# Norm weights on the queries alone, roots as the sigmoids' scale, and one eviction per head, in a two-layer hybrid decoder trunk

## The chip, the cores and the metric

The kernel runs on one core of a Trainium2 chip. A core has several engines with a queue each, and each queue is worked off in order: TensorE (PE, matrix products; its weight loads are shown as PEld), VectorE (DVE), ScalarE (ACT), GpSimd (POOL) and SyncE (SP). An engine that waits for a semaphore holds up all that stands behind in its queue. Transfers run beside the engines on 16 DMA engines, fed by queues that belong to the engine that issues them. The metric is the device time of one execution in microseconds (us), smaller is better.

## The reference

Two layers, each `x + mix @ w_out`, with a residual stream of 512 tokens by 2048 channels in 32 bit. All three parts of a layer read one projection of the normalised input: a short convolution, stick-breaking attention, and gated linear attention (GLA). The change is in the attention, 8 heads of 128 channels, which is this:

```python
q = _rmsnorm(sb_q.reshape(b, s, SB_HEADS, SB_HD), sb_qn_g)   # mean of squares over 128, + EPS, times a weight
k = _rmsnorm(sb_k.reshape(b, s, SB_HEADS, SB_HD), sb_kn_g)
# per block of 128 queries, strictly causal:
z = (q * hd ** -0.5) @ k.T
log_keep = where(mask, log_sigmoid(-z), 0)
later = reverse_cumsum(log_keep) - log_keep
w = where(mask, exp(log_sigmoid(z) + later), 0)
y_sb = (w @ v) * silu(sb_g)
```

Since exp(log_sigmoid(z) + later) is a sigmoid times a product of sigmoids, the kernel computes sigmoid(z) and sigmoid(-z) and a running product of the latter. The weights of the two norms differ by channel (`sb_qn_g`, `sb_kn_g`), the inverse roots by token and head.

## The kernel before

All matrix products are carried by pairs of half-precision numbers, a high part and the rest, with three products for each (high by high, high by low, low by high). Every weight column block of 256 columns is loaded in 32 bit (`fetch`, L346 to L360, issued from GpSimd), squared and summed for a scale (`wmax`, L366 on ScalarE), and split into the two halves (L435 and L442, or L485 and L486 for the blocks that use a product scheme with seven smaller products, `project_quick`, L749). Those steps are given a high priority.

The attention is a loop over j = 0 to 3 (L1277), two heads a pass, in each layer. A pass projects the values, the gate, the queries and the keys for 256 columns. `project_gate` and the keys' projection use `project_quick`, whose parts leave PSUM in pieces (L778 to L792). For the queries and then the keys (L1298) the pass
- copies the projection to SBUF (`raw`; one buffer for the queries),
- sums the squares of each token and head on ScalarE (L1318, eight pairs of instructions),
- forms the inverse roots of eight columns on VectorE in `rsqrt_bits` (L208): the scaled sum (L211), a first guess by integer arithmetic (L213) and three Newton steps of three instructions (L216 to L218), and then a scaling by the projection's unit `u` (L1324),
- multiplies in place: the queries by their roots in one instruction (L1327), the keys by their roots and by the channels' weights `kg` in eight instructions, one for each token tile and head (L1332); `kg` holds both norms' weights, so the queries have none,
- splits the product into the two halves (`qp`, one buffer; L1336 on ScalarE, L1337 on VectorE) and transposes each by a DMA issued from SyncE (L1341).

`attend` (L1214) then appends four steps to a list: the scores of the two heads and their values. `go` (L1210) takes the next of them off the list at fixed places of the following pass (after its values, its gate, its queries and its keys), and after the last pass in the second half of the convolution (`conv_in` and `conv_out`, L1346). The scores of a head are in two PSUM chunks (`CHUNKS`, L40): the query tiles 3 and 2 with 512 and 384 columns, and the tiles 0 and 1 with 128 and 256. For each chunk there are the products (L1226), the mask on the diagonal blocks (L1230), sigmoid(-z) and sigmoid(z) over the whole chunk with a scale that is the same for all queries (`nzun`, `zun`; L1234, L1236), a running product for each tile (L1239), their product (L1241), the split (L1244, L1245) and the transposes (L1247). The values of a head accumulate in one PSUM bank (L1263), which is evicted in two halves, one for each chunk (L1270); there is one such bank. `mixsplit` (L866) splits the result and sends it to DRAM (L879), and `mixload` (L881, L887, on SyncE) brings it back, in six loads, when the last pass is over.

The order of the instructions on each engine isn't the order of the text. A planner runs the program on a clock of its own before it is built, and an engine takes the instruction that is ready on that clock, with the earlier in the text or the higher priority first. The first stage up to L655 alone is ordered by hand. On the chip that order is fixed: where a transfer takes longer than on the planner's clock, the engine waits.

Of the kernel before, what the change touches and what calls it, by code (L numbers as in the profile page):

```python
# [17 lines left out]
P = 128  # L18
# [18 lines left out]
TWICE = ("wm", "wgm", "wq", "ws", "wp", "vu", "bm", "bsmix", "gsmix", "lr", "xr0", "xrm", "xrt", "xtot", "xrstd", "xrs")  # L37


CHUNKS = ((((3, 0), (2, 512)), (3, 2)), (((0, 0), (1, 128)), (0, 1)))  # L40
# [3 lines left out]
def hybrid_trunk(ctx, tc, x, norm_g, w_in, conv_w, conv_b, sb_qn_g, sb_kn_g,  # L44
# [163 lines left out]
    def rsqrt_bits(dst, src, scale, n, tag):  # L208

        m = sm(n, tag + "rm")  # L210
        V.tensor_scalar(m, src, scale, EPS, ALU.mult, ALU.add)  # L211
        r = sm(n, tag + "r0")
        V.tensor_scalar(r.bitcast(I32), m.bitcast(I32), -0.5, float(0x5F375A86), ALU.mult, ALU.add)  # L213
        t = sm(n, tag + "rt")
        for i in range(3):
            V.tensor_tensor(t, r, r, ALU.mult)  # L216
            V.scalar_tensor_tensor(t, t, -0.5, m, ALU.mult, ALU.mult)
            V.scalar_tensor_tensor(dst if i == 2 else r, t, 1.5, r, ALU.add, ALU.mult)  # L218
# [68 lines left out]
    def layer_consts():  # L287
# [3 lines left out]
        for l in range(depth):  # L291
# [11 lines left out]
            V.tensor_scalar(gq[:, 0:1], gq[:, 0:1], gq[:, 1:2], 2.0 ** -10, ALU.mult, ALU.mult)  # L303
# [353 lines left out]
    for l in range(depth):  # L657
# [556 lines left out]
        def attend(j, qT, kT, vh, vl, vu, g, s_):  # L1214
# [3 lines left out]
            def scores(hh):  # L1218

                th[hh] = wk([P, 2, 10, P], "th", 2, F16)  # L1220
                for n, (qtiles, _) in enumerate(CHUNKS):
# [12 lines left out]
                    S.activation(a, z[:, :zw], AF.Sigmoid, scale=nzun[:, l:l + 1])  # L1234
                    w = wk([P, zw], "zw")
                    S.activation(w, z[:, :zw], AF.Sigmoid, scale=zun[:, l:l + 1])  # L1236
# [12 lines left out]
            def values(hh):  # L1249
# [17 lines left out]
                for n, (_, cols) in enumerate(CHUNKS):  # L1267
                    q0 = min(cols)
                    a = op[:, 2 * n:2 * n + 2, :]
                    V.scalar_tensor_tensor(y[:, q0:q0 + 2, :], a[:, ::-1, :] if cols[0] > cols[1] else a, vu[:, 1:2],  # L1270
                                           g[:, hh, q0 * P:(q0 + 2) * P].rearrange("p (t c) -> p t c", c=P),
                                           ALU.mult, ALU.mult)
# [4 lines left out]
        for j in range(4):  # L1277
# [20 lines left out]
            for gain in (None, kg[:, l, :]):  # L1298
                raw = []

                def dst():
                    raw.append(wk([P, NT, GW], *(("raw", 1) if gain is None else ("kT",))))
                    return raw[0]
# [6 lines left out]
                sq = sm(8, "qs")  # L1310
                for b in range(2):
# [4 lines left out]
                    for i in range(4):  # L1316
                        cs = slice(i * P, (i + 1) * P)
                        S.activation(e[:, cs], rb.rearrange("p a c -> p (a c)")[:, cs], AF.Square,  # L1318
                                     accum_out=sq[:, 4 * b + i:4 * b + i + 1])
# [4 lines left out]
                V.tensor_scalar(rs, rs, u, None, ALU.mult)  # L1324
                if gain is None:
                    r8 = raw.rearrange("p a (h c) -> p (a h) c", c=P)
                    V.tensor_tensor(r8, r8, rs.rearrange("p (a o) -> p a o", o=1).to_broadcast([P, 8, P]), ALU.mult)  # L1327
                else:
                    for t in range(NT):
                        for hh in range(2):  # L1330
                            rp = raw[:, t, hh * P:(hh + 1) * P]
                            V.scalar_tensor_tensor(rp, rp, rs[:, 2 * t + hh:2 * t + hh + 1], gain, ALU.mult, ALU.mult)  # L1332

                top = 2.0 ** 10 if gain is None else 1.0
# [4 lines left out]
                nT_ = wk([P, 2, NT, 2, P], "kT" if qkT else "qT", dt=F16)  # L1339
# [4 lines left out]
            attend(j, *qkT, vh, vl, vu, g, s_)  # L1344
# [86 lines left out]
```

## Time and profile before

| | us |
|---|---|
| median of 3 runs | 1716.04 (1715.94 to 1717.55) |
| the profiled execution | 1717.69 |
| its span, first to last instruction | 1715.9 |
| TensorE busy | 1669.9 |
| VectorE busy | 1331.3 |
| ScalarE busy | 1129.1 |
| GpSimd busy | 239.2 |

The span is one execution as the hardware profiler recorded it. A row of a view names the engine, the line of the kernel, the operation, what is written and read, and its shape; a wait is put down to what ended it. The granted clock is the share of its full clock that TensorE was given. Views used here: the page (busy shares), the list of waits, windows (busy time of each engine in a stretch), the order of time on one engine, and groups of instructions by line. A TensorE that is busy is not always at its peak: matmuls overlap, and their recorded durations do too.

### The profile page before, as it was taken

How to read it: one execution, taken by the hardware profiler on the slowest of the kernel's cores; microseconds unless marked ns; L12 is line 12 of the kernel's file. 1: busy time of each engine (PE TensorE's matmuls, PEld its weight loads, DVE VectorE, ACT ScalarE, POOL GpSimd, SP SyncE). 2: the span in 40 equal slices, each digit the busy share in tenths (PEclk: the TensorE clock that was granted, in tenths of full speed). 3: DMA queues.
4: the chain of work that ended last, by engine and by line, in shares of the span. 5: the costliest groups of instructions: out<-in, count | busy, mean ns of one | idle time of the engine just before them, and what ended most of it. 6: DMA issues, size and time to landing. Idle time of an engine off the chain costs nothing.

```text
span 1715.9 us, 36876 instructions
## 1 busy us (share of the span) xinstructions
PE 1669.9 (97%) x15642; PEld 1298.4 (76%) x15642; DVE 1331.3 (78%) x2327; ACT 1129.1 (66%) x1619; POOL 239.2 (14%) x286
## 2 busy tenths in 40 slices
PE   7999999999999989999989999999999999899999
PEld 5644548989898964799976455689898889548998
DVE  8975889877878767785688677997786888677883
ACT  7667677767666656666665676776765767565662
POOL 1211111111111111001122101121111111101110
PEclk9999999999999999999999999999999999999999
DMA  7233323566766686245543332446666667753441
GB/s 251 83 114 98 99 64 99 145 116 152 136 149 139 147 233 164 77 150 181 186 103 108 116 102 75 118 123 125 148 136 105 146 132 150 201 153 108 162 151 50
DMA packets 181478, 227.26 MB, mean 132 GB/s; under 512 B 94194, under 2 KB 141628, under 8 KB 180800
## 3 DMA queue, kind: packets, MB, share of 16 engines
q0 software_dynamic: 60352, 168.83, 34.4%
q1 hardware_dynamic: 111952, 46.61, 14.4%
q10 hardware_dynamic: 9008, 9.45, 1.7%
q8 instruction: 122, 2.00, 0.5%
q14 instruction: 44, 0.36, 0.1%
HBM read 179.65 MB, written 14.68 MB: 113 GB/s over the span
## 4 chain that ended last, share of the span: by engine, by line
PE 73%; DVE 12%; DMA 7%; ACT 4%; issue 3%; POOL 0%; DVEq 0%; ACTq 0%
PE psp L767 13%; PE psp L674 8%; PE psp L675 8%; PE psp L673 8%; PE psp L685 7%; PE psp L684 7%; PE psp L683 7%; PE psp L814 6%; PE psp L764 3%; DMA st<-in_w_in_dram 2%; DVE wl L486 2%; DMA th<-za 2%; DMA kT<-qp 2%; ACT junk L366 1%; DVE wl L442 1%
## 5 line engine op out<-in xcount | busy, mean ns | idle before, releaser
L366 ACT ACTIVATE junk<-st 128x2048 uint8<-128x2048 f32 x150 | 285.1, 1901 | 44.1 <-DMA st<-in_w_in_dram 42.8
L442 DVE SCALAR_TENSOR_TENSOR wl<-st,ws,wh 128x2048 f16<-128x2048 f32 x102 | 239.2, 2347 | 80.7 <-ACT wh L435 80.7
L435 ACT ACTIVATE wh<-st,ws 128x2048 f16<-128x2048 f32 x100 | 199.3, 1998 | 105.4 <-PE psp L674 47.1
L684 PE MATMUL psp<-wl,m 128*128 128x256 f16 x960 | 261.7, 273 | 0.0
L683 PE MATMUL psp<-wh,m 128*128 128x256 f16 x960 | 261.7, 273 | 0.0
L685 PE MATMUL psp<-wh,m 128*128 128x256 f16 x960 | 261.7, 273 | 0.0
L485 ACT ACTIVATE wh<-st,ws 128x1024 f16<-128x1024 f32 x150 | 167.6, 1143 | 120.5 <-DVE st L506 57.7
L486 DVE SCALAR_TENSOR_TENSOR wl<-st,ws,wh 128x1024 f16<-128x1024 f32 x150 | 189.6, 1279 | 27.4 <-ACT wh L485 27.3
L355 POOL DMA_DIRECT2D st<-in_w_in_dram x114 | 102.2, 900 | 436.0 <-DVE wl L442 319.4
L683 PE MATMUL psp<-wh,x 128*128 128x256 f16 x512 | 139.6, 273 | 0.0
L684 PE MATMUL psp<-wl,x 128*128 128x256 f16 x512 | 139.6, 273 | 0.0
L685 PE MATMUL psp<-wh,x 128*128 128x256 f16 x512 | 139.6, 273 | 0.0
L675 PE MATMUL psp<-x,wl 128*128 128x512 f16 x352 | 134.4, 382 | 2.2 <-DVE zun L186 2.2
L674 PE MATMUL psp<-x,wh 128*128 128x512 f16 x352 | 134.4, 382 | 0.0
L673 PE MATMUL psp<-x,wh 128*128 128x512 f16 x352 | 134.0, 381 | 0.0
L673 PE MATMUL psp<-m,wh 128*128 128x512 f16 x352 | 133.9, 380 | 0.0
L674 PE MATMUL psp<-m,wh 128*128 128x512 f16 x352 | 133.9, 380 | 0.0
L675 PE MATMUL psp<-m,wl 128*128 128x512 f16 x352 | 133.9, 380 | 0.0
L675 PEld LDWEIGHTS <-wl 128*128 128x128 f16 x704 | 69.2, 98 | 85.0 <-DVE wl L442 2.7
L673 PEld LDWEIGHTS <-wh 128*128 128x128 f16 x704 | 69.2, 98 | 81.5 <-issue 3.1
L380 POOL PARTITION_ALL_REDUCE wgm<-wm x75 | 40.0, 533 | 648.2 <-ACT junk L366 633.6
L674 PEld LDWEIGHTS <-wh 128*128 128x128 f16 x704 | 69.2, 98 | 80.8 <-issue 2.3
(427 smaller groups left out, 4042.2 us busy)
## 6 DMA issues: line engine op xcount, KB each, us to landing
st<-in_w_in_dram POOLq DMA_DIRECT2D x114, 1024.0 KB, 8.4
st<-in_w_out_dram POOLq DMA_DIRECT2D x32, 1024.0 KB, 7.4
st<-st POOLq DMA_DIRECT2D x18, 512.0 KB, 8.3
st<-in_w_in_dram SPq DMA_DIRECT2D x6, 1024.0 KB, 12.0
mixd<-g POOLq DMA_DIRECT2D x24, 256.0 KB, 7.7
x<-in_x_dram SPq DMA_DIRECT2D x4, 1024.0 KB, 4.9
qT<-in_x_dram ACTq DMA_DIRECT2D x8, 512.0 KB, 3.8
qT<-xs ACTq DMA_DIRECT2D x8, 512.0 KB, 3.9
```

What stands on the lines that cost most here:

```text
L366: sq = S.activation(junk(HK * GW).rearrange("p (k n) -> p k n", k=HK), staged[i][h], AF.Square, accum_out=peak[i][:, h:h + 1])
L435: hi = S.activation(wh[:, :, :GW], staged[i][h], AF.Copy, scale=scales[i])
L442: V.scalar_tensor_tensor(wl[:, :, :GW], staged[i][h], scales[i], wh[:, :, :GW], ALU.mult, ALU.subtract)
L485: hi = S.activation(h_, b, AF.Copy, scale=sc)
L486: V.scalar_tensor_tensor(l_, b, sc, h_, ALU.mult, ALU.subtract)
L673: T.matmul(o, wh[:, kk, cs], xh[:, :, k, :], start=st_, stop=False)
L674: T.matmul(o, wh[:, kk, cs], xl[:, :, k, :], start=False, stop=False)
L675: mm = T.matmul(o, wl[:, kk, cs], xh[:, :, k, :], start=False, stop=en)
L683: T.matmul(o, ah[:, t, k, :], wh[:, kk, :n], start=st_, stop=False, skip_group_check=True)
L684: T.matmul(o, ah[:, t, k, :], wl[:, kk, :n], start=False, stop=False, skip_group_check=True)
L685: return T.matmul(o, al[:, t, k, :], wh[:, kk, :n], start=False, stop=en, skip_group_check=True)
L767: mm = T.matmul(o[:, t * P:(t + 1) * P], a[p_][:, t, kk, :], w[q_][:, kk, :], start=st_, stop=en, skip_group_check=True)
```

## The change

It has four parts.

1. The norms' weights move from the keys to the queries. The queries are multiplied by `kg` alone, in one instruction for all heads and tiles (the same 128 columns repeated), and no longer by their roots. The keys are multiplied by their roots alone, also in one instruction.
2. The queries' inverse roots become the scale of the sigmoids, which is one number for each partition, and a partition of the scores is a query. Roots, unit and scale are put together in `qz`: eight columns for sigmoid(-z) and eight for sigmoid(z). The sigmoids are therefore taken tile by tile, four tiles a head, where they were taken by chunk. Constants of powers of two are shifted to keep the half-precision range (`2.0 ** -21`, `2.0 ** -14`, `2.0 ** 25`).
3. The scaled sums of queries and keys lie in one tile of 16 columns, and one Newton chain is run on it, when the keys' sums are there.
4. The second chunk of scores has its tiles in the order 1, 0, so that the four tiles of a head's values lie in the order 3, 2, 1, 0 in their bank, and one instruction evicts them.

```diff
-CHUNKS = ((((3, 0), (2, 512)), (3, 2)), (((0, 0), (1, 128)), (0, 1)))
+CHUNKS = ((((3, 0), (2, 512)), (3, 2)), (((1, 0), (0, 256)), (1, 0)))
...
-    def rsqrt_bits(dst, src, scale, n, tag):
-
-        m = sm(n, tag + "rm")
-        V.tensor_scalar(m, src, scale, EPS, ALU.mult, ALU.add)
+    def rsqrt_bits(m, tag):
+
+        n = m.shape[-1]
         r = sm(n, tag + "r0")
         V.tensor_scalar(r.bitcast(I32), m.bitcast(I32), -0.5, float(0x5F375A86), ALU.mult, ALU.add)
         t = sm(n, tag + "rt")
         for i in range(3):
             V.tensor_tensor(t, r, r, ALU.mult)
             V.scalar_tensor_tensor(t, t, -0.5, m, ALU.mult, ALU.mult)
-            V.scalar_tensor_tensor(dst if i == 2 else r, t, 1.5, r, ALU.add, ALU.mult)
+            V.scalar_tensor_tensor(r, t, 1.5, r, ALU.add, ALU.mult)
+        return r
...
-                    S.activation(a, z[:, :zw], AF.Sigmoid, scale=nzun[:, l:l + 1])
                     w = wk([P, zw], "zw")
-                    S.activation(w, z[:, :zw], AF.Sigmoid, scale=zun[:, l:l + 1])
+                    for m, dst in ((0, a), (8, w)):
+                        for t, o in qtiles:
+                            ts_ = slice(o, o + (t + 1) * P)
+                            S.activation(dst[:, ts_], z[:, ts_], AF.Sigmoid,
+                                         scale=qz[:, m + 2 * t + hh:m + 2 * t + hh + 1])
...
-                for n, (_, cols) in enumerate(CHUNKS):
-                    q0 = min(cols)
-                    a = op[:, 2 * n:2 * n + 2, :]
-                    V.scalar_tensor_tensor(y[:, q0:q0 + 2, :], a[:, ::-1, :] if cols[0] > cols[1] else a, vu[:, 1:2],
-                                           g[:, hh, q0 * P:(q0 + 2) * P].rearrange("p (t c) -> p t c", c=P),
-                                           ALU.mult, ALU.mult)
+                V.scalar_tensor_tensor(y, op[:, ::-1, :], vu[:, 1:2], g[:, hh, :].rearrange("p (t c) -> p t c", c=P),
+                                       ALU.mult, ALU.mult)
...
-            for gain in (None, kg[:, l, :]):
+            sq, rm = sm(16, "qs"), sm(16, "qrm")
+            for n in range(2):
...
                 V.tensor_scalar(u2, u, u, 1.0 / P, ALU.mult, ALU.mult)
-                rs = sm(8, "qr")
-                rsqrt_bits(rs, sq, u2, 8, "q")
-                V.tensor_scalar(rs, rs, u, None, ALU.mult)
-                if gain is None:
-                    r8 = raw.rearrange("p a (h c) -> p (a h) c", c=P)
-                    V.tensor_tensor(r8, r8, rs.rearrange("p (a o) -> p a o", o=1).to_broadcast([P, 8, P]), ALU.mult)
+                V.tensor_scalar(rm[:, 8 * n:8 * n + 8], sq[:, 8 * n:8 * n + 8], u2, EPS, ALU.mult, ALU.add)
+                r8 = raw.rearrange("p a (h c) -> p (a h) c", c=P)
+                if not n:
+                    qu = sm(1, "qu")
+                    V.tensor_scalar(qu, u, nzun[:, l:l + 1], 2.0 ** 25, ALU.mult, ALU.mult)
+                    by = kg[:, l, :].rearrange("p (o c) -> p o c", o=1)
                 else:
-                    for t in range(NT):
-                        for hh in range(2):
-                            rp = raw[:, t, hh * P:(hh + 1) * P]
-                            V.scalar_tensor_tensor(rp, rp, rs[:, 2 * t + hh:2 * t + hh + 1], gain, ALU.mult, ALU.mult)
+                    rs = rsqrt_bits(rm, "q")
+                    qz = sm(16, "qz")
+                    V.tensor_scalar(qz[:, :8], rs[:, :8], qu, None, ALU.mult)
+                    V.tensor_scalar(qz[:, 8:], qz[:, :8], -1.0, None, ALU.mult)
+                    V.tensor_scalar(rs[:, 8:], rs[:, 8:], u, None, ALU.mult)
+                    by = rs[:, 8:].rearrange("p (a o) -> p a o", o=1)
+                V.tensor_tensor(r8, r8, by.to_broadcast([P, 8, P]), ALU.mult)
+
+                top = 2.0 ** 10 if n else 2.0 ** -14
```

More of the change, by code (lines that the diff above doesn't have):

```diff
@@ L33 @@
 AHEAD = (8, 17, 21)
-TWICE = ("wm", "wgm", "wq", "ws", "wp", "vu", "bm", "bsmix", "gsmix", "lr", "xr0", "xrm", "xrt", "xtot", "xrstd", "xrs")
-CHUNKS = ((((3, 0), (2, 512)), (3, 2)), (((0, 0), (1, 128)), (0, 1)))
+TWICE = ("wm", "wgm", "wq", "ws", "wp", "vu", "bm", "bsmix", "gsmix", "lr", "xr0", "xrm", "xrt", "xtot", "xrstd", "xrs", "qz")
+CHUNKS = ((((3, 0), (2, 512)), (3, 2)), (((1, 0), (0, 256)), (1, 0)))
 @with_exitstack
@@ L1297, in hybrid_trunk @@
             qkT = []
-            for gain in (None, kg[:, l, :]):
+            sq, rm = sm(16, "qs"), sm(16, "qrm")
+            for n in range(2):
                 raw = []
                 def dst():
-                    raw.append(wk([P, NT, GW], *(("raw", 1) if gain is None else ("kT",))))
+                    raw.append(wk([P, NT, GW], *(("kT",) if n else ("raw", 1))))
                     return raw[0]
```

12 lines of the change are left out of this document (5 added, 7 removed).

## The prediction

> **What bounds the kernel now.** I read the page's busy shares first, then who TensorE waited for, then the windows around its two longest waits inside the attention, and last the queues that feed them (VectorE, ScalarE, SyncE) in order of time.
>
> ```profile
> span 1715.9 us, 36876 instructions
> ...
> PE 1669.9 (97%) x15642; PEld 1298.4 (76%) x15642; DVE 1331.3 (78%) x2327; ACT 1129.1 (66%) x1619; POOL 239.2 (14%) x286
> ```
>
> TensorE is busy for 97% of the span. What it loses is the difference, 46 us, and the change adds or removes no matmul. So the change is worth only what it does to TensorE's waits, of which these rows are the ones near it (total us, times, longest):
>
> ```profile
> PE psz L1226 <- DMA kT<-qp: 11.0, 2, 5.9
> PE psp L764 <- ACT g L785: 5.5, 6, 1.9
> ...
> PE psm L1263 <- DVE e L1270: 3.6, 1, 3.6
> ...
> PE psz L1226 <- ACT zw L1236: 1.4, 1, 1.4
> ```
>
> The first row is the scores' first matmul waiting for the transposed keys, once in each layer. The windows at these two places, two ordinary passes of the head loop, and the stretch before the first of the waits show what they cost (columns: length, busy time of each engine with counts, TensorE's granted clock, DMA share, GB/s):
>
> ```profile
> 594.40:624.00 29.60, 28.95 (x355) 25.96 (x353) 28.90 (x62) 22.02 (x38) 6.01 (x8) 1.00 0.75 181
> 1265.00:1350.00 85.00, 82.95 (x910) 75.09 (x908) 64.81 (x116) 52.65 (x81) 14.04 (x15) 1.00 0.79 147
> 634.28:640.15 5.87, 0.00 (x1) 0.00 (x1) 0.35 (x1) 0.00 (x0) 0.00 (x0) 0.86 1.23 159
> 640.15:645.35 5.20, 5.20 (x14) 1.85 (x14) 0.00 (x0) 1.06 (x1) 0.00 (x0) 0.50 0.93 317
> 1487.06:1492.22 5.16, 0.00 (x1) 0.00 (x0) 1.50 (x1) 0.00 (x0) 0.00 (x0) 0.96 1.21 193
> 1492.22:1495.30 3.08, 3.08 (x9) 1.17 (x9) 0.00 (x0) 0.00 (x0) 0.00 (x0) 0.51 1.03 291
> 420.00:505.00 85.00, 84.73 (x937) 76.92 (x935) 68.46 (x120) 58.66 (x89) 14.21 (x16) 1.00 0.68 147
> ```
>
> An ordinary pass has little to give: TensorE is busy 84.73 or 82.95 of 85.00 us, at a clock of 1.00. At the last pass (j = 3) of each layer TensorE stands still for 5.87 and 5.16 us, and then runs at half clock for 5.20 and 3.08 us, which loses another 5.20 x 0.50 + 3.08 x 0.49 = 4.1 us. Together 15.1 us: that is the prize. The Trainium skill, "TensorE: Matmul & The Clock Gate" (section "Why this matters for your kernels"), asks for no idle gap over about 3 us, since a longer one brings the half clock. The trace agrees here: both gaps are longer and both have it. By that rule a gap cut to under 3 us would save its clock part whole. The rows say so without it: the pass from 1265 loses 2.05 us in short waits and keeps its clock of 1.00.
>
> **Why the keys are late.** VectorE in the last pass of layer 0: the queries' product (L1327), the keys' Newton chain from its start (L211) to its end (L1324), a weight split (L442) that got in ahead, and the keys' eight products (L1332); under it the keys' products of layer 1.
>
> ```profile
> 597.01 0.17 DVE L218 SCALAR_TENSOR_TENSOR qr<-qrt,qr 128x8 f32<-128x8 f32 x1
> 597.21 0.17 DVE L216 TENSOR_TENSOR qrt<-qr 128x8 f32<-128x8 f32 x1
> ...
> 598.68 1.23 DVE L1327 TENSOR_TENSOR raw<-raw,qr 128x1024 f32<-128x1024 f32 x1
> ...
> 612.48 0.22 DVE L211 TENSOR_SCALAR qrm<-qs,qu 128x8 f32<-128x8 f32 x1
> ...
> 616.63 0.23 DVE L1324 TENSOR_SCALAR qr<-qr,wu 128x8 f32<-128x8 f32 x1
> 616.77 2.35 DVE L442 SCALAR_TENSOR_TENSOR wl<-st,ws,wh 128x2048 f16<-128x2048 f32 x1
> 619.03 2.19 DVE L1332 SCALAR_TENSOR_TENSOR kT<-kT,qr,kg 128x128 f32<-128x128 f32 x8
> ...
> 1471.80 2.18 DVE L1332 SCALAR_TENSOR_TENSOR kT<-kT,qr,kg 128x128 f32<-128x128 f32 x8
> ```
>
> ScalarE at that time: the last square of the keys, two weight splits with a copy between, the squares of the next weights, which wait 2.87 us for their DMA, and behind them the keys' half-precision copy (L1336).
>
> ```profile
> 610.51 0.29 ACT L1318 ACTIVATE e<-kT 128x128 f32<-128x128 f32 x1
> ...
> 612.96 1.14 ACT L485 ACTIVATE w7h<-st,ws 128x1024 f16<-128x1024 f32 x1
> ...
> 614.61 1.99 ACT L435 ACTIVATE wh<-st,ws 128x2048 f16<-128x2048 f32 x1
> 616.50 0.36 ACT L782 ACTIVATE qT<-psp 128x256 f32<-128x256 f32 x1
> 617.17 2.00 ACT L435 ACTIVATE wh<-st,ws 128x2048 f16<-128x2048 f32 x1 [0.31 <-PE psp L764]
> 622.05 1.91 ACT L366 ACTIVATE junk<-st 128x2048 uint8<-128x2048 f32 x1 [2.87 <-DMA st<-in_w_in_dram]
> ...
> 623.96 1.04 ACT L1336 ACTIVATE qp<-kT 128x1024 f16<-128x1024 f32 x1
> ```
>
> And SyncE, which issues the transposes: the queries' pair, four loads of the mix (two at 617.17, two at 622.41), the keys' two transposes; the last row is, over all of L1341's transposes, the time from issue to landing.
>
> ```profile
> 601.02 6.51 SPq L1341 DMA_TRANSPOSE qT<-qp  x2
> ...
> 617.17 0.94 SPq L887 DMA_DIRECT2D m<-mixd  x2
> ...
> 622.41 1.85 SPq L887 DMA_DIRECT2D m<-mixd  x2
> ...
> 625.02 8.40 SPq L1341 DMA_TRANSPOSE kT<-qp  x1
> ...
> 633.52 4.84 SPq L1341 DMA_TRANSPOSE kT<-qp  x1
> ...
> DMA to landing us min/median/max: 3.3/8.3/15.0
> ```
>
> The reader is to see a queue of three: the products end at 621.22, the copy at 625.00, and the two issues take 8.40 and 4.84 us, because the big mix loads have just gone into the same queue. The keys are there at 640.15; TensorE's order has the scores at 634.28. That place is the planner's estimate: it lies 13.06 us behind the products' end (634.28 - 621.22), and in layer 1 13.08 us (1487.06 - 1473.98).
>
> **The change, part by part.**
>
> *Queries' chain dropped, one chain of 16.* In each of the 8 passes VectorE loses ten small steps at a pitch of 0.20 us (597.01 to 597.21), 2.0 us, and one scaling by u, 0.23. The squared unscale and the scaled sums stay, one instruction each for queries and keys. Added are the queries' u (one column) and two rows of qz: at the 0.23 of L1324 at most 0.7. The queries' product still waits for its squares, because it writes over what they read; only the chain between is gone. So the queries go to SyncE about 2 us earlier, at some 599 instead of 601.02, and the copy of the keys, which needs their single buffer back, is released 2 us earlier. ScalarE's wait for that buffer (18.6 us in all) shrinks, beside TensorE's work:
>
> ```profile
> L1336 ACT ACTIVATE qp<-kT 128x1024 f16<-128x1024 f32 x8 | 8.4, 1053 | 21.8 <-DMA qT<-qp 18.6 <-DVE kT L1332 3.2
> ```
>
> *Keys' eight products become one.* 2.19 becomes the 1.23 of L1327 (same shape): 0.96 less. VectorE in all: 2.0 + 0.23 + 0.96 - 0.7 = 2.5 us a pass, 20 us of 1331. By itself this is hidden behind TensorE, worth nothing in passes 0 to 2.
>
> *What it does in pass 3.* VectorE is busy 28.90 of the 29.60 us before 624, so 2 us taken out at 597 come out of the backlog in front of 612.48. The squares end at 610.9 (610.51 + 0.29 and the read of the sum); the chain starts there, 1.6 us earlier, needs 2.0 us, the three small scalings 0.7, and I allow 0.4 for another step slipped in: about 614.0. The next weight split is ready at 612.96 + 1.14 = 614.10, so the keys' product runs just before or just after it: 614.0 + 1.23 = 615.2, or with a split of 1024 columns ahead of it (half of L442's 2.35 and a little, 1.3) 616.6. It ends between 615.2 and 616.6 instead of 621.22, in front of L442 either way. The copy then fits on ScalarE behind L782 (616.86) or behind the second L435 (619.17), and ends at 618 to 620.3, ahead of the squares that wait for a DMA. SyncE has issued the first two mix loads by 618.11 and its third is not ready before 622.41, so the planner should put the keys' transposes between them. Then they meet an emptier queue, as the queries did: second issue 1.6 us behind the first (6.51 us for both is the upper bound), 8.3 us to land, hence 628 to 630. The scores stand 13.06 us behind the product, at 628.3 to 629.7. A wait of 0 to 1.7 us is left; I take 1.5 a layer. Bounds from both sides: none left, and with the longest landing (15.0) 7 us, which is the present wait and more. The two mix loads that are now passed start up to 6.5 us later. Their first reader comes 60 us on, which covers that:
>
> ```profile
> L1150 ACT ACTIVATE m<-m,ratio x14: 706/1133/1148, 685.7 to 1543.4; 128x1024 f16<-128x1024 f16 x12, 128x512 f16<-128x512 f16 x2
> ```
>
> *Sigmoids.* Two chunks of 896 and 384 columns become four tiles of 512, 384, 256 and 128, twice each:
>
> ```profile
> L1236 ACT ACTIVATE zw<-psz,zun 128x896 f32<-128x896 f32 x16 | 16.0, 999 | 0.0
> ...
> L1236 ACT ACTIVATE zw<-psz,zun 128x384 f32<-128x384 f32 x16 | 9.4, 586 | 0.0
> ```
>
> 999 - 586 = 413 ns over 512 columns is 0.81 ns a column, and 0.28 us are fixed; four more instructions a head cost 1.1 us, or 0.7 where they overlap by 0.10 (614.61 + 1.99 against 616.50). Over 16 heads that is 11 to 18 us of ScalarE, which has 58.66 of 85 us filled. On TensorE's path it matters where a copy or a bank waits behind sigmoids: the seven waits of L785 and L1236 above. Each longer by 0.7 is 4.9 us, none longer is 0. The rows don't tell how many of L785's hang on sigmoids; with ScalarE two thirds full I take the lower third, 1.5. The rule that speaks against the change is in the Trainium skill, "ScalarE: Activation LUTs" (section "What ACT_TABLE_LOAD costs"): about 186 ns fixed, 93 more for a pointer operand. The trace agrees (0.28 with one). By the page's figure the four cost 4 x 0.28 x 16 = 17.9 us, which is the upper end above.
>
> *Values evicted at once.*
>
> ```profile
> L1270 DVE SCALAR_TENSOR_TENSOR e<-psm,vu,g 128x256 f32<-128x256 f32 x32 | 13.9, 477 | 10.2 <-ACT e L1318 8.4 <-PE psm L1263 1.8
> ...
> L877 DVE SCALAR_TENSOR_TENSOR g<-e,bsmix,g 128x512 f16<-128x512 f32 x12 | 8.9, 744 | 0.0
> ```
>
> 13.9 / 16 = 0.87 us a head become about the 0.74 of a 512-wide step. The bank is free when the last half is read, in both versions; the first half could start earlier before, but only the end counts. Between -3.6 (TensorE's wait for it gone) and +0.5 (the 477 ns of the half that can no longer run early), I take 0. The turned order of the last two tiles moves no work.
>
> **Sum.** Waits -11.0 + 3.0; clock -4.1; sigmoids +1.5; the rest 0: -10.6 us. The profiled execution took 1717.69 (span 1715.9 and 1.8 around it) and lies 1.65 above the median of 1716.04; taken off the median, **1705.5 us**.
>
> **Rivals.**
>
> *The wait stays.* The copy still ends up behind the squares, or the planner keeps all four mix loads first. SyncE is then free at 622.41 + 1.85 = 624.26, 0.76 us earlier than 625.02. For it: L366 is high in the planner's order and blocks ScalarE in both layers. Against it: the product comes over 4 us earlier. 1716 - 1.5 + 1.5 = 1716 us.
>
> *Slower: the scores move up, the transposes don't.* TensorE's order follows the planner's clock, not the chip's. If it moves the scores up with the product (to about 629) while on the chip the keys land at 640.15 - 0.76 = 639.4, the wait is about 10 us instead of 5.87, and 9.5 instead of 5.16: +8.7, and up to 3 more at half clock. It decides against the change as soon as the scores move up by more than 0.76 us without the transposes passing the mix loads. For it: the planner's 13.06 us were 5.87 too short already. With the sigmoids 1716 + 8.7 + 3 + 1.5 = 1729 us; half of that move gives 1722.
>
> *ScalarE eats the gain.* All of the 0.7 to 1.1 us a head reaches TensorE: 11 to 18 instead of 1.5, so 1715 to 1722 us. For it: ScalarE runs in order, with TensorE's copies behind the sigmoids. Against it: an ordinary pass leaves it 26 us idle.
>
> **Chances.** Forecast 0.50 (its own range 1698 to 1711: from all 15.1 and part of the L1270 wait gone, to half the waits left); wait stays 0.22; scores move up 0.16; ScalarE 0.12. A difference of 0.2%, 3.4 us, is about what a measurement of this kernel can tell from none. Faster: 0.50 and 0.05 of the two rivals near 1716, whose other waits shift with a new order: 0.55. Same 0.18, slower 0.16 and 0.11 of those two: 0.27. Leaving out no more than 2 in 10, the range runs from 1697 to 1724.
>
> **What would show it.** Right: the wait of L1226 for the transposed keys goes from 11.0 to under 4 us, the clock stays at 1.00 in the last passes, SyncE's keys stand between the second and the third mix load, L1336 for keys waits less than 18.6 us for the queries' transposes, VectorE is some 20 us less busy and ScalarE 11 to 18 more. Wrong: that wait unchanged or longer, or new waits of TensorE on sigmoids.

## The result, and the profile after

The changed kernel took 1739.28 us (median of 4 runs, 1737.37 to 1747.79), the kernel before beside it 1715.99 (4 runs, 1714.73 to 1717.55): ratio 1.0145, 95% interval 1.011 to 1.018. It is 23 us slower; 11 us faster was forecast. A later series gave 1743.30 and 1.0147 [1.0123, 1.0172].

The page of the changed kernel's profiled execution (1737.37 us), span and busy shares:

```profile
span 1735.6 us, 36801 instructions
...
PE 1672.7 (96%) x15642; PEld 1298.0 (75%) x15642; DVE 1311.7 (76%) x2191; ACT 1140.0 (66%) x1683; POOL 239.8 (14%) x286
```

VectorE has 19.6 us less to do and ScalarE 10.9 more, as forecast (20; 11 to 18). TensorE does the same work in 2.8 us more, and idles 62.9 us of the span instead of 46.0. So the loss lies in its waits. The view of waits, TensorE's rows of the attention (total us, times, longest):

```profile
PE psz L1226 <- DMA kT<-qp: 29.2, 4, 12.6
...
PE psp L764 <- ACT g L785: 3.7, 4, 1.5
...
PE psz L1226 <- ACT zw L1238: 2.3, 1, 2.3
...
PE psm L1266 <- DVE e L1270: 0.6, 1, 0.6
```

The wait that was to fall from 11.0 to 3.0 us rose to 29.2; of the others shown, the score banks' (1.4 before) rose by 0.9 us and two fell. In a second profile of the same kernel (e17 below) two of them are larger: 7.4 us for the score banks and 5.1 for the eviction. Windows around its three long pieces and behind two of them (columns as in the prediction: length, busy times, granted clock, DMA share, GB/s):

```profile
631.31:641.86 10.55, 0.00 (x1) 0.00 (x0) 1.27 (x1) 0.00 (x0) 0.00 (x0) 0.70 1.04 179
641.86:647.86 6.00, 5.99 (x20) 2.41 (x20) 0.00 (x0) 0.00 (x0) 0.00 (x0) 0.68 1.47 184
1391.25:1396.85 5.60, 0.00 (x1) 0.00 (x0) 0.00 (x0) 0.00 (x0) 0.00 (x0) 0.98 1.40 79
1494.19:1506.77 12.58, 0.01 (x1) 0.01 (x1) 2.35 (x1) 0.58 (x1) 0.00 (x0) 0.69 1.14 178
1506.77:1512.77 6.00, 6.00 (x15) 2.23 (x15) 0.00 (x0) 0.00 (x0) 0.00 (x0) 0.51 0.95 200
```

The two old gaps, 5.87 and 5.16 us, are 10.55 and 12.58, and layer 1's third pass has a new one of 5.60. In layer 0 the scores stand at 631.31, 2.97 us earlier than before, and the keys come at 641.86, 1.71 later. SyncE in that pass, in order of time:

```profile
597.01 9.93 SPq L1343 DMA_TRANSPOSE qT<-qp  x2
617.87 0.99 SPq L887 DMA_DIRECT2D m<-mixd  x2
621.45 3.16 SPq L1343 DMA_TRANSPOSE kT<-qp  x1
624.71 6.79 SPq L887 DMA_DIRECT2D m<-mixd  x2
631.59 12.95 SPq L1343 DMA_TRANSPOSE kT<-qp  x1
```

The planner put one of the keys' transposes between the second and the third mix load, as the prediction had it, and the other behind the fourth. Neither met an emptier queue: the second took 12.95 us to issue, and the first, which TensorE's wait was for, landed only 20.38 us after its issue. The chain in order of time (start, us):

```profile
621.45 20.38 DMA kT<-qp
```

The queries' pair now goes out 4.0 us earlier (597.01 against 601.02) and takes 9.93 us instead of 6.51. VectorE between the keys' squares and their product:

```profile
612.16 0.27 DVE L1321 TENSOR_SCALAR qrm<-qs,qu 128x8 f32<-128x8 f32 x1 [0.88 <-ACT e L1317]
...
613.59 1.28 DVE L486 SCALAR_TENSOR_TENSOR w7l<-st,ws,w7h 128x1024 f16<-128x1024 f32 x1
...
614.87 0.74 DVE L877 SCALAR_TENSOR_TENSOR g<-e,bsmix,g 128x512 f16<-128x512 f32 x1
...
616.03 2.35 DVE L442 SCALAR_TENSOR_TENSOR wl<-st,ws,wh 128x2048 f16<-128x2048 f32 x1
...
619.11 1.22 DVE L1334 TENSOR_TENSOR kT<-kT,qr 128x1024 f32<-128x1024 f32 x1
620.25 2.34 DVE L442 SCALAR_TENSOR_TENSOR wl<-st,ws,wh 128x2048 f16<-128x2048 f32 x1
```

And ScalarE, with the squares of the next weights ahead of the keys' last square:

```profile
609.85 1.90 ACT L366 ACTIVATE junk<-st 128x2048 uint8<-128x2048 f32 x1
...
611.74 0.29 ACT L1317 ACTIVATE e<-kT 128x128 f32<-128x128 f32 x1
```

The chain begins late, because it waits for that square, and three larger steps slip into it. The product ends at 620.33, 0.9 us earlier than before and not 4.6 to 6. Two more rows bear on the rest. The first, of VectorE's waits, is 0.3 us in the kernel before. The second is ScalarE's copy of the keys in layer 1's third pass, waiting for the queries' late transposes to give their buffer back, from which the new gap of 5.60 us follows:

```profile
DVE st L506 <- DMA st<-st: 9.2, 4, 5.9
```

```profile
1386.40 1.06 ACT L1338 ACTIVATE qp<-kT 128x1024 f16<-128x1024 f32 x1 [12.10 <-DMA qT<-qp]
```

The st wait is for L503, which adds one quarter of a weight block to another by a transfer in GpSimd's queue, behind the weight loads. It now lands late: at most 22.0 us after its issue, against 14.7 before.

### The profile page after: what moved, and what is told of

Same layout as the page of the kernel before. It is cut to its first block, busy times and chain, and to the rows that moved or that the text cites. A ratio compares the mean times of both kernels' runs of the same rounds, so it can differ in the third digit from the quotient of the medians.

```text
span 1735.6 us, 36801 instructions
## 1 busy us (share of the span) xinstructions
PE 1672.7 (96%) x15642; PEld 1298.0 (75%) x15642; DVE 1311.7 (76%) x2191; ACT 1140.0 (66%) x1683; POOL 239.8 (14%) x286
## 4 chain that ended last, share of the span: by engine, by line
PE 78%; DVE 8%; DMA 7%; ACT 4%; issue 2%; POOL 0%; ACTq 0%; DVEq 0%; POOLq 0%
PE psp L767 15%; PE psp L684 8%; PE psp L685 8%; PE psp L683 8%; PE psp L675 8%; PE psp L674 8%; PE psp L673 8%; PE psp L814 6%; PE psp L764 4%; DMA kT<-qp 2%; DMA st<-in_w_in_dram 2%; ACT junk L366 2%; PE psm L1266 1%; DVE wl L486 1%; PE psz L1014 1%
## 5 line engine op out<-in xcount | busy, mean ns | idle before, releaser
L366 ACT ACTIVATE junk<-st 128x2048 uint8<-128x2048 f32 x150 | 285.1, 1901 | 33.7 <-DMA st<-in_w_in_dram 32.5
```

Source lines behind the costliest of these rows:

```text
L366: sq = S.activation(junk(HK * GW).rearrange("p (k n) -> p k n", k=HK), staged[i][h], AF.Square, accum_out=peak[i][:, h:h + 1])
```

## The experiments

In each, the edit is against the kernel named. Ratios are against the kernel before, run beside it on the same chip; 0.001 is 1.7 us. "kT" is TensorE's wait for the transposed keys, "st" VectorE's wait for L503, both in the profiled run. The series ran on different chips, so between them only ratios are compared. One profile is one execution, and not always near the median: e10's (1699.62 us) is its fastest run, e13's (1726.89) close to its slowest. Line numbers shift by a few with the edits.

| run | kernel | median us | ratio, 95% interval | kT us | st us |
|---|---|---|---|---|---|
| | before | 1715.99 | 1 | 11.0 | 0.3 |
| | changed | 1739.28 | 1.0145 [1.011, 1.018] | 29.2 | 9.2 |
| e17 | changed, again | 1743.30 | 1.0147 [1.0123, 1.0172] | 27.4 | 13.8 |
| e1 | before + tiled sigmoids | 1727.35 | 1.0054 [1.0032, 1.0076] | 14.0 | 0.3 |
| e2 | before + single eviction | 1719.15 | 1.0009 [0.9987, 1.0031] | 12.9 | 0.6 |
| e3 | changed, queries' own chain | 1741.16 | 1.0138 [1.0104, 1.0172] | 28.2 | 0.5 |
| e4 | changed, keys' pair before 3rd mix load | 1748.63 | 1.0177 [1.0144, 1.0209] | 34.1 | 11.5 |
| e5 | changed, keys' pair before all mix loads | 1726.41 | 1.0052 [1.0027, 1.0077] | 5.8 | 9.2 |
| e6 | e5, weight load behind the pair | 1720.72 | 1.0014 [0.9993, 1.0035] | 5.2 | 10.5 |
| e13 | changed, keys' pair behind 4 mix loads | 1719.57 | 1.0015 [0.999, 1.0039] | 10.4 | 8.1 |
| e11 | e6 + queries' own chain | 1709.84 | 0.9968 [0.9942, 0.9993] | none | none |
| e16 | e13 + queries' own chain | 1712.76 | 0.9969 [0.9951, 0.9987] | 2.6 | none |
| e9 | before, keys' pair before all mix loads | 1712.64 | 0.9969 [0.9944, 0.9994] | 6.8 | 0.3 |
| e7 | e9, weight load behind the pair | 1704.74 | 0.9916 [0.989, 0.9941] | none | none |
| e14 | e7, again | 1699.90 | 0.9901 [0.9876, 0.9926] | none | none |
| e10 | e7 + tiled sigmoids | 1708.18 | 0.995 [0.9921, 0.9979] | none | none |
| e15 | e7, queries sent early | 1720.29 | 1.0024 [0.9997, 1.0051] | 7.1 | 16.4 |

### Parts of the change alone

e1: in the kernel before, each sigmoid cut into tiles, with the common scale kept:

```diff
-S.activation(a, z[:, :zw], AF.Sigmoid, scale=nzun[:, l:l + 1])
+for t, o in qtiles:                       # and the same for w with zun
+    ts_ = slice(o, o + (t + 1) * P)
+    S.activation(a[:, ts_], z[:, ts_], AF.Sigmoid, scale=nzun[:, l:l + 1])
```

> The kernel before with one part of the change alone: sigmoids tile by tile (eight a head), with the old scale. Theory order (the loss of 23 us comes from TensorE's scores moving up while the keys' transposes land later, at the last pass of each layer): within 4 us of before, 1712 to 1720, the wait for transposed keys stays at about 11 us in 2 waits. Theory sigmoids (the extra ScalarE time reaches TensorE): 1727 to 1734, with new waits of TensorE on L785 or on the score banks.

1.0054: the sigmoids alone cost some 9 us. The median lies at the lower edge of the second theory's range, but not by the waits that it named. TensorE's:

```profile
PE psz L1226 <- DMA kT<-qp: 14.0, 2, 8.4
PE psm L1265 <- DVE e L1272: 6.7, 3, 2.8
PE psp L764 <- ACT g L785: 5.4, 6, 1.6
```

The waits on L785 (5.5 before) and on the score banks (1.4 before, none here) did not grow; those for the values' eviction (3.6 before) and for the keys did.

e2: the kernel before with the values' tiles in the new order, evicted by one instruction for both halves (`V.scalar_tensor_tensor(y, op[:, ::-1, :], ...)` instead of the loop over CHUNKS):

> The kernel before with the turned tile order and the single eviction alone. Theories order and collision: 1712 to 1720, the wait for the eviction (3.6 us before) 0 to 4 us. Theory eviction (a later release of the bank holds up the values): over 1722, with waits of TensorE on L1270 above 6 us.

1.0009: nothing that could be measured, as forecast.

### The keys' transposes and the mix loads

e4, in the changed kernel (`order(a, b)` puts a behind b on the same engine; `turned` holds the last pass's two transposes):

```diff
 for i in range(2):
-    nc.sync.dma_start(mix[i][:, :, ks, :], mixd[l][...])
+    back_ = nc.sync.dma_start(mix[i][:, :, ks, :], mixd[l][...])
+    if i or ks.start == 4:
+        for a in turned:
+            order(back_, a)
```

> The changed kernel with both transposes of the last pass's keys held together in SyncE's queue ahead of the third mix load. Theory order (the second transpose is late because two mix loads stand before it): it is issued at about 624 instead of 631.6 of layer 0, the two last-pass waits fall from 10.6 and 12.6 to under 6 each, 1720 to 1728. Theory collision (a transpose that is in flight with weight loads crawls, wherever it stands): its issue or landing still takes over 10 us and the waits stay above 8 each, 1733 to 1742.

1.0177: exactly the place that the prediction gave the pair, unsplit, and the slowest of all, above both ranges. The waits are those of theory collision (15.5 and 18.1 us at the two last passes). Its SyncE, and its wait:

```profile
625.17 0.99 SPq L888 DMA_DIRECT2D m<-mixd  x2
628.75 16.13 SPq L1348 DMA_TRANSPOSE kT<-qp  x2
644.98 9.27 SPq L888 DMA_DIRECT2D m<-mixd  x4
```

```profile
PE psz L1230 <- DMA kT<-qp: 34.1, 3, 18.1
```

The third to sixth mix loads had not been issued, and still the pair took 16.13 us to issue. So these loads are not what holds it there, and the splitting of the pair is not needed for the loss.

e5 is e4 without its `if`: all six mix loads behind the pair. e6 adds to e5 that the one weight load that would run beside the pair waits for it, since two of its elements are first written from the transposed keys:

```diff
 whole[i] = stage.tile([P, KT, GW], F32, tag="st", name=nm("st"))
+if i in (29, 67):
+    G.tensor_copy(whole[i][0:1, HK - 1:HK + 1, 0], held[-1][0:1, 1, 0, 0, 0:2])
```

> The changed kernel with the last pass's two keys' transposes held ahead of all six mix loads of the layer in SyncE's order, nothing else. Theory 1 (collision: transposes in flight together with the 2 MB weight load of GpSimd's queue make both crawl): they are issued by about 622 and 624, the weight load of 622.9 is in flight with them, both take 15 us or more, the waits for kT at the two last passes stay between 25 and 36 us together, time 1736 to 1750. Theory 2 (it is the mix loads in the same queue that hold the transposes, as the prediction had it): with nothing ahead of them they land by 630 to 632, the two waits fall below 8 us together, time 1712 to 1722.

> The same with one more edit: the weight load that would be in flight with the last pass's keys' transposes (both halves of it, one load a layer) first has two of its elements written by GpSimd from the transposed keys, so it can only be issued once they have landed. Theory 1: the transposes, alone, take about 4 us each as in the passes without a collision and land at 628 to 632; the waits for kT at the two last passes fall from about 30 to under 10 us together, the weight load takes 6 to 11 us instead of 21 and is in no later than 644, time 1715 to 1726. Theory 2: the same waits as without the edit, and the weights later on top, time no lower than the kernel without it. A third case: the transposes land early, and TensorE then waits for the later weights (L442 or L435 as the releaser) for as long as it gained.

e5, 1.0052: theory 2's waits (5.8 us), and a time between the two theories'. With nothing before them the two issues take 3.55 us together instead of 16.13, and the first transpose is there when TensorE comes for it, in layer 0. The second is not through before the weights flow: it lands 11.61 us after its issue. SyncE, and the chain in order of time:

```profile
639.13 3.55 SPq L1347 DMA_TRANSPOSE kT<-qp  x2
...
641.44 11.61 DMA kT<-qp
```

e6, 1.0014: holding the weight load back gains another 6 us, with intervals that overlap a little (in the kernel before, e9 to e14 below, 12 us without overlap). Of its 5.2 us of wait, 0.2 is at the last passes.

e13 restores the order that SyncE had in the kernel before: `order(a, back_)` for the first four mix loads, `order(back_, a)` for the last two.

> The changed kernel with the last pass's keys' pair of transposes held behind the first four mix loads, the order that SyncE had in the kernel before; nothing else. If the planner's splitting of the pair around the third and fourth load raised the waits from 11 to 29 us, they fall back to 11 plus the 3 us by which the scores stand earlier in each layer, 13 to 18 us together, and the time to 1722 to 1732. If any place behind loads costs as much once the scores have moved up, the waits stay at 25 to 36 us and the time at 1734 to 1745.

1.0015, below the lower end expected. The third pass of layer 1 has 7.3 of the 10.4 us of wait; at the two last passes it is 1.5 and 1.6 us. The edit did two things. In layer 0 the first transpose lands 13.8 us after its issue instead of 20.4, and the scores stand 12.4 us behind that issue (637.71 to 650.08) instead of 9.9 (621.45 to 631.31). So of the 9.1 us that the wait lost there, 6.6 are the transfer and 2.5 the planner's order.

The traces of these runs, and of e9 below, give that time for both last passes:

| run | mix loads ahead of the pair | weight load issued (layers 0 and 1) | first transpose, issue to landing, us |
|---|---|---|---|
| changed | 2 | 1.4 us after the pair | 20.4, 22.4 |
| e4 | 2 | 1.4 us after | 25.3, 27.9 |
| e5 | none | 1.4 us after | at most 6.2, 8.7 |
| before | 4 | 1.2 and 3.9 us ahead of it | 15.1, 11.6 |
| e13 | 4 | 1.2 and 1.6 us ahead | 13.8, 13.6 |
| e9 | none | 1.2 and 2.5 us ahead | 9.0, 8.1 |

Between e5 and e4 the weight load stands at the same distance, so the two mix loads ahead make the difference. The pair is slowest where it has both: mix loads ahead of it and the weight load close behind.

### The queries' transposes

e3, in the changed kernel: the queries get their own chain of eight back, and their product stands behind it.

```diff
+rs = rsqrt_bits(rm[:, 8 * n:8 * n + 8], "q")
 if not n:
     qu = ...
+    V.tensor_scalar(qz[:, :8], rs, qu, None, ALU.mult)
+    ready = V.tensor_scalar(qz[:, 8:], qz[:, :8], -1.0, None, ALU.mult)
...
-V.tensor_tensor(r8, r8, by.to_broadcast([P, 8, P]), ALU.mult)
+order(V.tensor_tensor(r8, r8, by.to_broadcast([P, 8, P]), ALU.mult), ready)
```

> The changed kernel with the single chain undone: the queries have their own chain of eight again, and their product stands behind it on VectorE, so their transposes leave 2 us or more later; all other parts stay. Theory collision (the earlier transposes meet the weights' transfers and both crawl): the new wait in pass 2 of layer 1 (5.6 us) is gone and the second issue of the queries' transposes takes 1.2 to 2 us again instead of 3.8 to 6.2; 1722 to 1732. Theory order: the last-pass waits stay, 10.6 and 12.6, since the keys are still ready before the third mix load; 1732 to 1740.

1.0138, no change that could be measured, though the wait of layer 1's third pass is gone and the "st" wait nearly so: SyncE still had the keys' pair among the mix loads, and at the two last passes the wait did not stay at 23.2 us, as theory order had it, but grew to 28.2. One fault hid the other. e11 makes the same edit in e6, where the keys' pair is mended:

> The changed kernel with both edits to the transfers, and the queries' inverse roots by a chain of eight of their own again with the queries' product behind it, so the queries' transposes leave 2 to 5 us later than in the change. If the early queries meeting the weight loads are what is left of the loss, the wait of 4.67 us for kT in layer 1's third pass goes and the time falls by 4 to 8 us to 1712 to 1717. If the sigmoids are what is left, it stays within 3 us of 1720.7.

0.9968, 8 us better than e6, with intervals that just meet: first case. e15 goes the other way, from e7 (below): the queries are multiplied by a constant row, their roots are left out with the chain that forms them, and a power of two is shifted, so that they leave early; all else of e7 is kept.

```diff
 if gain is None:
-    V.tensor_tensor(r8, r8, rs.rearrange(...).to_broadcast([P, 8, P]), ALU.mult)
+    V.tensor_tensor(r8, r8, kg[:, l, :].rearrange(...).to_broadcast([P, 8, P]), ALU.mult)
...
```

> The kernel before with the two edits to the transfers, and the queries multiplied by a constant row in place of their inverse roots, so that their transposes leave 2 to 5 us earlier, as in the change; the queries' inverse roots are left out of the computation, and VectorE is spared their chain of some dozen small instructions in each pass. If early queries by themselves are what the shared chain cost, their second transpose takes 4 to 8 us to issue in most passes and the time is 4 to 9 us above the same kernel with the roots. If leaving early is harmless, it is within 3 us of it or below.

1.0024 against e14's 0.9901, 21 us, over twice the most that was expected, although VectorE had less to do. TensorE's waits in e15, of which e14 has 0.2 us of the last and none of the others; then VectorE's and ScalarE's:

```profile
PE psz L1232 <- ACT zw L1242: 7.4, 3, 3.7
PE psz L1232 <- DMA kT<-qp: 7.1, 6, 3.3
...
PE psm L1269 <- DVE e L1276: 4.0, 1, 4.0
```

```profile
DVE st L509 <- DMA st<-st: 16.4, 3, 5.8
```

```profile
ACT wh L488 <- DVE st L509: 73.1, 16, 8.5
```

The last row is 57.2 us in e14. ScalarE waits 15.9 us more for VectorE, and VectorE 16.4 for the accumulating transfer. In all eight passes the queries' pair takes longer to issue, 5.74 to 10.30 us against 3.34 to 6.50 in e14. The waits read as a chain: the early transposes delay what stands in GpSimd's queue, the weight splits come late, and the sigmoids behind them on ScalarE too. Over all runs this wait is 8.1 to 16.4 us where the queries leave early (the changed kernel, e17, e4, e5, e6, e13, e15) and at most 0.6 where they leave late. The planner's order also moved in e15; how much of the 21 us that is, stays open.

### Both undone, and the kernel before mended

e16 is e13 with e3's edit. Tiled sigmoids, the keys' single product and the single eviction stay. e17 is the changed kernel itself.

> The changed kernel with both causes undone: the queries' inverse roots by their own chain again (their transposes leave later), and the last keys' pair behind the first four mix loads. Tile-wise sigmoids, one product for the keys and the single eviction stay. If the two causes are the whole loss, the wait of VectorE for st by the accumulating transfer (9.2 us in the change, none before) is gone, the waits for kT are 11 to 17 us, and the time is 1709 to 1717, that of the kernel before or a little under. If the sigmoids' 9 us stand beside them, 1720 to 1727.

> The changed kernel once more: 1736 to 1744, 1.011 to 1.018 of the kernel before, if its first four runs stand for it.

e16, 0.9969, is some 5 us faster than the kernel before and 31 faster than e17 (1.0147): with the two transfers mended the whole loss is gone, and more. That does not show that what is left of the change gains. The wait for the keys was to be 11 to 17 us and is 2.6, against 11.0 in the kernel before, so e16 has also mended a fault of the kernel before.

e9, e7 and e14 put the transfers' edits of e5 and e6 into the kernel before; e10 adds e1's tiled sigmoids to e7.

> The kernel before with one edit: the last pass's two keys' transposes ahead of all six mix loads of the layer in SyncE's order; the weight load is free to go. If the place in SyncE's queue was the whole of the wait, the two waits for kT (5.87 and 5.16 us) go as they did when the weight load was held as well: 1700 to 1708. If the weight load in flight with them matters too, the waits stay at 3 us or more each and the time lies at 1709 to 1718.

> The two edits (keys' transposes ahead of the mix loads, that weight load behind them) in the kernel before, whose scores stand later and whose sigmoids are whole. Theory 1: the transposes are issued at about 625 and land by 633, so the 5.87 and 5.16 us of wait and most of the half clock behind them go: 1702 to 1710 against 1716. Theory 2: nothing gained, 1714 to 1722.

> The kernel before with the two edits to the transfers, once more and with more runs: 0.989 to 0.995 of the kernel before if its first three runs told the truth, above 0.997 if they were lucky.

> The kernel before with both edits to the transfers (keys' transposes ahead of the mix loads, that weight load behind them) and the sigmoids cut into tiles of one scale, as in the change, but with the common scale and the old chains. If the sigmoids' own instructions cost time in every pass (the first runs gave 9.3 us for them, part of it as waits for kT), the time is 6 to 10 us above the same kernel with whole sigmoids, 1710 to 1716. If their 9.3 us came from where the scores met the late keys, it is within 3 us of it, 1702 to 1708.

The order alone (e9) gave 0.9969, with 6.8 us of wait left, its second case; with the weight load held too, 0.9916 and, repeated, 0.9901: 1699.90 us, the fastest kernel here. e14's SyncE and GpSimd in the last pass:

```profile
626.50 2.61 SPq L1348 DMA_TRANSPOSE kT<-qp  x2
629.28 3.24 SPq L891 DMA_DIRECT2D m<-mixd  x6
```

```profile
631.23 0.18 POOL L354 CAST st<-kT 1x2 f32<-1x2 f16 x1 [2.00 <-DMA kT<-qp]
631.70 1.80 POOL L358 DMA_DIRECT2D st<-in_w_in_dram  x2 [0.30 <-POOL st L354]
```

Both issues take 2.61 us instead of the 8.40 + 4.84 of the kernel before, the keys are there 4.7 us after the first, and TensorE waits for them no more. One run of e7 took 3548.91 us and isn't in its ratio. The tiled sigmoids on top (e10) cost 0.0034 against e7 and 0.0049 against e14, 6 to 8 us, though e10's interval overlaps both.

e11 and e7 are alike in their transfers: in both the pair goes first, the weight load is held, the queries leave late, and TensorE has no wait for the keys. What differs is the rest of the change (tiled sigmoids, one product for the keys, one eviction), and it costs 0.0052 against e7 and 0.0067 against e14, 9 to 12 us, with intervals that don't overlap. By e10 the tiled sigmoids are most of it; nothing in the rest was seen to gain.

### The transfers alone

Nothing of the reference is computed in these two; they only move data of the disputed sizes and write zeros. e8 has idle engines, e12 also starts the pair a little into the weight load and has phases with busy engines.

> Not the computation (all of it is left out, the output is zeros): only transfers of the sizes in dispute, in five phases kept apart by VectorE and repeated three times: two transposes of 128x1024 alone; a 2 MB weight load on GpSimd's queue alone; both together; the weight load together with a 2 MB load on SyncE's queue; transposes and weight load one behind the other on SyncE's queue. Theory 1: alone the pair lands within 8 us and the load within 11 us; together both take more than the sum of the two alone (over 19 us); two ordinary loads take no more than twice one; one behind the other on one queue takes no more than the sum. Theory 2: together takes no longer than the sum of the two alone.

> Not the computation (all of it is left out, the output is zeros): transfers of the sizes in dispute alone, twice over. A pair of transposes issued about 2 us into a 2 MB weight load; the same with ScalarE, VectorE and TensorE busy on other tiles; a transpose, two loads of 512 KB and a transpose in SyncE's queue with the weight load in GpSimd's, idle engines and busy ones; the load and the pair alone beside busy engines. If transposes and weight load slow each other by themselves, one of the mixed phases takes over 18 us with idle engines (the load alone took 9, the pair 4.5). If the engines' own traffic is needed for it, only the busy ones do. If none does, what made them crawl in the changed kernel is not in these transfers.

Chain in order of time (start, us): the pair's second transpose alone, the weight load's second half alone, and that transpose with the load started beside it (e8); the same with the pair issued 1.3 us into the load (e12):

```profile
22.18 3.14 DMA kT<-qp
...
27.34 8.05 DMA st<-in_w_in_dram
...
37.44 9.93 DMA kT<-qp
```

```profile
28.14 11.07 DMA kT<-qp
```

The pair took 4.5 us alone (20.80 to 25.32) and 11.2 with the load beside it (36.15 to 47.37), the load 9.1 and 10.4. Issued into the running load, the pair took 12.5 us, its second issue 7.1. So a load in large packets (2.10 MB in 544) makes the pair, in small ones (0.52 MB in 2112), last about as long as itself. But neither case exceeded the two durations added (13.6 us), and theory 1's over 19 failed. Theory 2 held. With busy engines the pair took 13.9 and 15.3 us. The longest form was a transpose, two loads and a transpose in SyncE's queue beside the weight load: 14.2 us with idle engines, 17.8 and 18.5 with busy ones, once just over the 18 us that e12 had set as its mark.

## Why the prediction was wrong

*The step that failed* is "Then they meet an emptier queue ... hence 628 to 630". It read the issue times of 8.40 and 4.84 us as the price of standing behind four mix loads, and took the place between the second and third for an emptier one. There two loads were still ahead and the weight load came 1.4 us behind, and the first transpose took 20.4 us to land where 8.3 had been put; the keys came at 641.86. e4 gave the place pure: 25.3 us, and 34.1 us of wait in all. Only ahead of all mix loads was it short (9.0 us or less in e5, e9 and e14). In the sum, the waits' term of -11.0 + 3.0 came out as +18.2, and the clock's -4.1 did not come at all: the mean granted clock fell from 0.992 to 0.987. The rival that came nearest is the second ("the scores move up, the transposes don't"): the scores moved 2.97 us, past its deciding point of 0.76, though one of the transposes did pass two loads. Its price of 1722 to 1729 missed the landing's own delay and the queries'.

*The missing term* is the queries' transposes. The prediction sent them 2 us earlier and gave that no cost. In the last pass of layer 0 they left 4.0 us earlier, 2.1 us behind the issue of a weight load instead of 6.2. Sending them late again gains 8 us (e6 to e11, e13 to e16), and sending them early costs 21 (e14 to e15), part of which may be the planner's order.

*The product's time* failed too: 615.2 to 616.6 forecast, 620.33 measured. The 0.4 us for steps slipped in was 4.4 (1.28 + 0.74 + 2.35), and the squares ended 1.2 us later than assumed, since L366 went before the last of them. As e14 shows with the product where it always was, this earliness was not needed.

*The sigmoids* were mis-sized: 1.5 us forecast, 9 (e1) and 6 to 8 (e10) measured. The instructions' own cost was right (10.9 us on ScalarE, the lower end of 11 to 18); their effect on TensorE was most of it, and not the lower third. In e1 it came by way of the evictions and keys. In e10, where no wait for the keys is left, the way isn't shown.

*What held*: VectorE -19.6, ScalarE +10.9, the eviction at nothing, and the prize. It was put at 15.1 us; e14 takes 1 - 0.9901 = 17 us [13, 21], by moving transfers and nothing of the arithmetic. The half clock behind a long gap also came back: 6.00 us at 0.68 and at 0.51 above. By the Trainium skill, "TensorE: Matmul & The Clock Gate" (section "Why this matters for your kernels"), gaps over about 3 us are to be avoided; the trace agrees (in e9 a gap of 3.27 us is followed by 4.00 us at 0.60), and where e14 has no such gap in the attention its mean clock is 0.996, against 0.992 before and 0.987 in the changed kernel.

## What to carry to other kernels

A step made earlier sends its transfers earlier: look up which load is in flight at the new time, in every pass and not only where the wait stands. Send small-packet transfers that are on the critical path ahead of the big loads: here the keys took 4.7 us with all loads held behind them, 12 to 15 behind four loads, and 20 to 28 among them. Where a planner orders the queue, an explicit order is cheap; it was worth 17 us here, and the arithmetic saved was worth nothing that could be measured. Two faults at one place can hide each other, so undo them singly and together before a verdict on either.

## What had not been expected of the hardware

With transposes and a weight load in flight together, the transfers of the full kernel slowed to less than a quarter for some microseconds. Windows of the changed kernel (last pass of layer 0, and layer 1's third pass, where no mix load is near), and of the kernel before at the first of these times:

```profile
626.00:634.00 8.00, 5.31 (x33) 2.97 (x31) 3.27 (x6) 3.91 (x5) 0.40 (x1) 1.00 1.21 79
1372.00:1378.00 6.00, 6.00 (x58) 5.38 (x56) 4.31 (x20) 2.30 (x3) 2.87 (x3) 1.00 1.33 51
```

```profile
626.00:634.00 8.00, 8.00 (x51) 4.80 (x49) 3.75 (x9) 5.23 (x5) 0.40 (x1) 1.00 1.09 349
```

At a higher DMA share (1.21 and 1.33 against 1.09) the rate is 79 and 51 GB/s instead of 349. From issue to landing the weight load of the last pass takes, in the changed kernel and in the one before (the view of its two issues):

```profile
DMA to landing us min/median/max: 21.0/22.3/23.5
```

```profile
DMA to landing us min/median/max: 9.3/12.0/14.8
```

The transfers alone never did this, with idle engines or busy ones (18.5 us at most). What in the full kernel brings it on is not settled. Transposes and a weight load in flight at once are not enough: in e5 the load follows the pair at the same distance, and it lands in

```profile
DMA to landing us min/median/max: 8.6/9.8/10.9
```

In the last pass two mix loads stood ahead of the pair where it happened (the changed kernel, e4). In layer 1's third pass there were none, but a store of the mix and the accumulating transfer of L503 joined (18.3 and 22.0 us to landing), and neither was among the transfers alone.
